# A decoder step on one Trainium2 core: 50 tokens leave the dense expert sum instead of 42, in two gather groups

## The chip, the cores and the metric

The kernel runs on one core of one Trainium2 chip. The metric is the device time of one execution in microseconds (us). The kernel before takes 2029.45 us (median of three runs, 2025.85 to 2030.77). The core's engines are TensorE (PE, matmuls; its weight loads are shown apart as PEld), VectorE (DVE), ScalarE (ACT), GpSimd (POOL) and SyncE (SP). SP's instructions here are DMA issues alone. Each engine works through its own list in order.

## The reference

One layer is computed for 256 prompt tokens and 8 sample tokens (264 in all), width 2048: a projection, a recurrent and an attention half, an output projection with layer norm, then a retrieval layer over 16384 experts. In the retrieval layer every token has 8 heads of 16 experts, 128 in all:

```python
def peer_block(xb, wq, sub_k1, sub_k2, u_tab, v_tab):
    ...
    e = (jnp.take_along_axis(i1, si // PEER_TOPK, axis=-1) * N_KEYS
         + jnp.take_along_axis(i2, si % PEER_TOPK, axis=-1))
    g = jax.nn.softmax(sv, axis=-1)
    ug = u_tab[e]
    act = jax.nn.gelu(jnp.einsum('nd,nhkd->nhk', xb, ug, preferred_element_type=jnp.float32))
    vg = v_tab[e]
    out = jnp.einsum('nhk,nhkd->nd', (g * act).astype(vg.dtype), vg, preferred_element_type=jnp.float32)
```

Both tables have 16384 rows of 2048 fp32 values, 128 MB each. The output is the layer norm of 2^0.25 · x plus this sum, with the keys, values and states of the first half.

## The kernel before

**Two ways to the same sum.** For the first `ND` = 222 tokens ("dense columns") the kernel multiplies with the whole tables: 128 blocks of 128 experts, in each an `up` product (activations of these experts for all dense tokens), gelu, a multiplication with a gate matrix that is zero for experts a token did not choose, and a `down` product. The last `NG` = 42 tokens (34 prompt and 8 sample tokens) are gathered: each stands on `REP` = 3 partitions, each partition has `NJ` = 43 of its 128 experts, and 43 × 2 indirect DMAs of 128 half rows (512 KB) fetch the rows of u, 43 × 2 more those of v.

**Precision by pairs.** A weight block of 512 KB arrives as `raw`; ACT casts its high part (L101, L809) and DVE subtracts to get the low part (L104, L814). Both go with one 444-column matmul (high weights with the high and low half of the operand, 2 × 222 columns: L1202 in `up`, L1247 in `down`) and one 222-column matmul (low weights, high half: L1203, L1249). Each `up` has 16 such pairs, and so has each `down`. In the first six blocks (`NAT`) `up` is plain fp32, on 222 columns (L938).

**The step loop.** Step s does `up(s)`; from s = 34 on (v = s − 34) also `down(v)`, and both add a block's result to `x1` with two DVE sums (`add`, L1255). Steps 0 to 33 run `up` alone; in steps 4 to 20 the gate matrices are made besides, from selections on ACT and DVE and 128-column products, and stored to HBM (`Gd`, 14 stores, L1153). Steps 34 to 127 run both; after them 34 steps run `down` alone (`last_step`), here called the tail. Every eight steps `load_g` loads the gate matrices of eight blocks, 14 DMAs of 64 KB each (L1224).

**Gathers beside the steps.** `gathered()` is a generator, called after each step of v = 0 to 118 as often as a credit of `GRATE` = 1.7 a step allows. A call issues one gather on POOL and uses the one of three calls before (`GDELAY`): for u a dot product with the token's row (L1414), for v an accumulation (L1426, L1428), each one DVE instruction on 1024 elements. At its end 16 matmuls with a selection matrix (L1434) sum the three partitions of each token, and two DVE sums (L1435) add them to `x1`. At its beginning SP loads the expert numbers (`exf`), gate values (`gat`) and the token's rows (`xrep`), 15 DMAs (L1383 to L1385), and DVE makes gather indices of them (`eix`, L1389, L1390).

**What sets the order.** Nothing is reordered: each engine runs the instructions in the order of the code. A weight buffer `raw` (six of them) is loaded again once its low part is subtracted; a pair of high and low parts has one of five slots. SP's DMAs take one of eight completion semaphores in turn, and a DMA waits until the one before it on that semaphore has landed.

Of the kernel before, what the change touches and what calls it, by code (L numbers as in the profile page):

```python
# [47 lines left out]
TRATE = 4  # L48
LEAD = 4
GWAIT = 2  # L50
GRATE = 1.7
GDELAY = 3
EPS = 1e-5
LAM0 = 0.8 - 0.6 * math.exp(-0.0)
# [4 lines left out]
def _build(tc, I, O):  # L59
# [3 lines left out]
    with ctx:  # L63
# [52 lines left out]
        def pmisc(shape):  # L116
            return psum.tile(shape, F32, name="misc", bufs=mmb[0])
# [832 lines left out]
        NEGF = -3.0e38  # L950
        ex = pool_in(ctx, "exp", 1)
        blocks = [(a, 16) for a in range(0, NE, 16)]
        Gd = [dram.tile([128, 128, n], F32, name=f"Gd{a}") for a, n in blocks]
        Ed = dram.tile([SEQ - ND, 128], F32, name="Ed")
        gd = dram.tile([SEQ - ND, 128], F32, name="gd")
        Es = dram.tile([2, NB, 128], F32, name="Es")
# [149 lines left out]
        def tokens(tt):  # L1106
# [19 lines left out]
            for bk, (a0, n) in enumerate(blocks):  # L1126
# [3 lines left out]
                for t4 in range(0, n, 4):  # L1130
# [16 lines left out]
                    def product(a=a, b=b, st=st, t4=t4, w=w, n=n, bk=bk):  # L1147
                        p = psum.tile([128, 4, 128], F32, name="acc2")
                        for q in range(w):
                            nc.tensor.matmul(p[:, q, :], b[:, q, :], a[:, q, :], start=True, stop=True)  # L1150
                        nc.scalar.copy(st[:, :, t4:t4 + w], p[:, :w].rearrange("p t i -> p i t"))
                        if t4 + w == n:
                            nc.sync.dma_start(Gd[bk], st)  # L1153

                    prev.append(product)
                    yield
# [209 lines left out]
        gp = pool_in(ctx, "gath", 1)  # L1366


        eix = gp.tile([128, 2, NJ], I32, name="eix")
        gat = gp.tile([128, NJ], F32, name="gat")  # L1370

        def gathered():
            exf = gp.tile([128, NJ], F32, name="exf")
            selM = cload("selM", [128, NG], pool=gp)
            xrep = gp.tile([128, DM], F32, name="xrep")

            for t in (exf, gat, xrep):
                nc.gpsimd.memset(t, 0.0)
# [10 lines left out]
            nc.vector.tensor_scalar(eix[:, 0], exf, 2.0, None, op0=OP.mult)  # L1389
            nc.vector.tensor_scalar(eix[:, 1], exf, 2.0, 1.0, op0=OP.mult, op1=OP.add)  # L1390
            dots = gp.tile([128, 2, NJ], F32, name="dots")
            yield

# [6 lines left out]
            todo = [(j, a) for j in range(NJ) for a in range(2)]  # L1400

            def ahead(tab, use):
                got = []
                for n in range(len(todo) + GDELAY):
                    if n < len(todo):
                        j, a = todo[n]
                        got.append(rows(tab, a, j))
                    if n >= GDELAY:
                        j, a = todo[n - GDELAY]
                        use(got.pop(0), j, a, slice(a * 1024, (a + 1) * 1024))  # L1410
                    yield

# [76 lines left out]
def _arrays(inp):  # L1489
# [86 lines left out]
```

## Time and profile before

| | us |
|---|---|
| median of three runs | 2029.45 (2025.85 to 2030.77) |
| the profiled execution | 2028.38 |
| its span, first to last instruction | 2026.6 |
| PE busy, PEld busy | 1957.9, 1825.5 |
| DVE busy | 1597.7 |
| ACT busy | 970.9 |
| POOL busy | 343.6 |

The profile is of one execution. Busy time counts an engine's own instructions; a matmul's end is modelled, and matmuls overlap in their pipeline, so the time between starts tells more than the duration of one. The table of stretches gives, for any part of the span, busy time of each engine, the clock granted to TensorE (1.00 is 2.4 GHz, 0.50 is 1.2 GHz), the mean busy share of the 16 DMA engines, and the bytes they moved.

### The profile page before, as it was taken

What the parts mean: (1) busy time and instruction counts of PE and PEld (TensorE: products, weight loads), DVE (VectorE), ACT (ScalarE), POOL (GpSimd) and SP (SyncE); (2) the same over time, 40 slices, a digit from 0 to 9 for tenths busy, and PEclk for the clock granted to TensorE, in tenths of its full rate; (3) what the DMA queues carried; (4) which work ended last, traced back from release to release, by engine and by line L of the source; (5) the groups of instructions that cost most, each with busy time, mean ns of one, the idle gap of its engine ahead of it and who ended that gap; (6) DMA issues with size and microseconds to landing.
All of it is one profiled execution on the core that took longest, in us unless ns stands there. A gap on an engine that the chain in (4) does not pass through costs nothing.

```text
span 2026.6 us, 37121 instructions
## 1 busy us (share of the span) xinstructions
PE 1957.9 (97%) x13874; PEld 1825.5 (90%) x13874; DVE 1597.7 (79%) x2907; ACT 970.9 (48%) x1600; POOL 343.6 (17%) x429
## 2 busy tenths in 40 slices
PE   8999999998999999999999999999999999998995
PEld 8889788797889999999999999999999999997895
DVE  6534656776599888678888888888788888889877
ACT  4224655543211897555454444445554444443443
POOL 2000000004000001012222222222122222223012
PEclk9999899999999999999999999999999999999998
DMA  8899598753344567788988889898788898989661
GB/s 310 298 354 332 184 340 314 271 175 131 125 140 145 192 240 253 262 280 315 322 300 317 301 315 320 287 329 315 269 311 318 300 323 289 327 300 337 230 211 61
DMA packets 179811, 544.18 MB, mean 269 GB/s; under 512 B 22538, under 2 KB 51298, under 8 KB 177586
## 3 DMA queue, kind: packets, MB, share of 16 engines
q1 hardware_dynamic: 150960, 446.92, 63.5%
q0 software_dynamic: 27952, 94.85, 13.2%
q8 instruction: 109, 1.79, 0.3%
q14 instruction: 70, 0.57, 0.1%
q10 hardware_dynamic: 720, 0.05, 0.0%
HBM read 522.19 MB, written 19.54 MB: 267 GB/s over the span
## 4 chain that ended last, share of the span: by engine, by line
PE 79%; DVE 9%; DMA 5%; ACT 4%; issue 2%; SPq 1%; POOL 0%; POOLq 0%; DVEq 0%; ACTq 0%
PE mm L1202 19%; PE acc L1247 19%; PE mm L1203 9%; PE acc L1249 9%; PE mm L938 8%; PE mm L300 3%; PE mm L301 2%; PE mm L302 2%; DMA cv<-in_ck 2%; DVE lo L104 1%; PE acc L1150 1%; DMA cv<-in_cv 1%; PE acc L561 1%; PE acc L640 1%; DVE xrep L1428 1%
## 5 line engine op out<-in xcount | busy, mean ns | idle before, releaser
L104 DVE TENSOR_TENSOR lo<-raw,hi 128x1024 fp32r<-128x1024 f32 x273 | 332.8, 1222 | 77.5 <-ACT hi L101 76.5
L1247 PE MATMUL acc<-w,hi 128*128 128x444 f32 x1224 | 392.8, 374 | 0.0
L101 ACT CAST hi<-raw 128x1024 fp32r<-128x1024 f32 x273 | 284.2, 1045 | 194.6 <-PE acc L1247 141.4
L1202 PE MATMUL mm<-A,hi 128*128 128x444 f32 x1176 | 375.7, 375 | 0.0
L1249 PE MATMUL acc<-w,lo 128*128 128x222 f32 x1224 | 323.7, 264 | 4.6 <-DVE lo L814 4.6
L1203 PE MATMUL mm<-A,lo 128*128 128x222 f32 x1176 | 310.7, 264 | 3.1 <-DVE lo L104 3.1
L1247 PE MATMUL acc<-w,xl 128*128 128x444 f32 x824 | 266.5, 374 | 0.0
L1255 DVE TENSOR_TENSOR M<-M,acc 128x444 f32<-128x444 f32 x256 | 158.2, 618 | 116.5 <-PE acc L1249 108.2
L1202 PE MATMUL mm<-A,xl 128*128 128x444 f32 x776 | 248.4, 375 | 0.0
L1247 PEld LDWEIGHTS acc<-w,hi 128*128 128x128 f32 x1224 | 229.4, 187 | 17.1
L1249 PEld LDWEIGHTS acc<-w,lo 128*128 128x128 f32 x1224 | 233.2, 191 | 8.0 <-DVE lo L814 7.8
L1202 PEld LDWEIGHTS mm<-A,hi 128*128 128x128 f32 x1176 | 220.8, 188 | 16.1
L1203 PEld LDWEIGHTS mm<-A,lo 128*128 128x128 f32 x1176 | 224.7, 191 | 3.3 <-DVE lo L104 3.3
L1249 PE MATMUL acc<-w,xl 128*128 128x222 f32 x824 | 218.8, 266 | 2.8 <-DVE xl L814 2.8
L1203 PE MATMUL mm<-A,xl 128*128 128x222 f32 x776 | 205.2, 264 | 0.0
L101 ACT CAST xl<-raw 128x1024 fp32r<-128x1024 f32 x139 | 145.1, 1048 | 120.3 <-PE acc L1247 100.1
L1396 POOL DMA_INDIRECT ug<-in_u,eix x86 | 118.6, 1379 | 387.7 <-DVE ug L1414 366.7
L104 DVE TENSOR_TENSOR xl<-raw,xl 128x1024 fp32r<-128x1024 f32 x139 | 170.6, 1230 | 15.3 <-ACT xl L101 15.1
L1396 POOL DMA_INDIRECT ug<-in_v,eix x86 | 118.9, 1382 | 344.6 <-DVE xrep L1428 309.4
L1232 ACT CAST w<-ac 128x222 fp32r<-128x222 f32 x128 | 48.5, 379 | 265.5 <-DVE ac L1229 247.9
L1247 PEld LDWEIGHTS acc<-w,xl 128*128 128x128 f32 x824 | 154.9, 188 | 11.5
L1249 PEld LDWEIGHTS acc<-w,xl 128*128 128x128 f32 x824 | 157.4, 191 | 4.8 <-DVE xl L814 4.7
(382 smaller groups left out, 4008.9 us busy)
## 6 DMA issues: line engine op xcount, KB each, us to landing
raw<-in_uT SPq DMA_DIRECT2D x256, 512.0 KB
raw<-in_vt SPq DMA_DIRECT2D x256, 512.0 KB
raw<-in_w_in SPq DMA_DIRECT2D x74, 512.0 KB
cv<-in_ck SPq DMA_DIRECT2D x64, 512.0 KB
cv<-in_cv SPq DMA_DIRECT2D x64, 512.0 KB
raw<-in_wq SPq DMA_DIRECT2D x32, 512.0 KB
Gd<-stage SPq DMA_DIRECT2D x14, 1024.0 KB
gt<-Gd SPq DMA_DIRECT2D x224, 64.0 KB
```

Of the source, the lines that this page charges most:

```text
L101: nc.scalar.copy(hi, raw)
L104: (eng or nc.vector).tensor_tensor(lo, raw, hi, op=OP.subtract)
L300: nc.tensor.matmul(p, hi, xh[:, c], start=c == 0, stop=False)
L301: nc.tensor.matmul(p, hi, xl[:, c], start=False, stop=False)
L938: nc.tensor.matmul(p, w[c // 8][:, c % 8, :], x1[:, c, :n], start=c == 0, stop=c == NC_ - 1)
L1202: nc.tensor.matmul(p, hi[:, c % 8, :], x1s[:, c], start=c == 0, stop=False)
L1203: nc.tensor.matmul(p[:, 0, :], lo[:, c % 8, :], x1s[:, c, 0], start=False, stop=c == NC_ - 1)
L1232: nc.scalar.copy(W[k][:, 0], ac[:, :ND])
L1247: nc.tensor.matmul(p[:, c, :2 * ND].rearrange("p (b t) -> p b t", b=2), hi[:, b % 8, :], w, start=i == 0, stop=False)
L1249: nc.tensor.matmul(p[:, c, :ND], lo[:, b % 8, :], w[:, 0], start=False, stop=i == 7)
L1255: nc.vector.tensor_tensor(a, a, p[:, :, b * ND:(b + 1) * ND], op=OP.add)
L1396: nc.gpsimd.indirect_dma_start(out=t, out_offset=None, in_=tab, in_offset=bass.IndirectOffsetOnAxis(ap=eix[:, a, j:j + 1], axis=0))
```

## The change

The number of gathered tokens goes from 42 to 50, and the dense columns from 222 to 214; `NE`, the padded count of gate columns, stays 224. The gathered tokens form two groups: the 42 of before (now `t0` = 222), three partitions each, 43 experts a partition; then eight prompt tokens (`t0` = 214) on 16 partitions each, eight experts a partition. The groups run one after the other in one generator, so the second has its own loads (16 × 3 DMAs), indices, 16 + 16 gathers and reduction. The credit is 2.2 a step while s < 128 and 0.7 in the tail. The gate matrices lie in one HBM tensor in the order in which they are loaded: a store writes runs of 512 B, and one DMA of 7 KB a partition loads eight blocks.

```diff
-NG = 42
+NG = 50
 ND = T - NG
-REP = 128 // NG
-NJ = -(-128 // REP)
+
+GROUPS = [(a, n, 128 // n, -(-128 // (128 // n))) for a, n in ((T - 42, 42), (ND, NG - 42))]
+NJ = max(g[3] for g in GROUPS)
...
-GRATE = 1.7
+GRATE = 2.2
+GTAIL = 0.7
...
-        Gd = [dram.tile([128, 128, n], F32, name=f"Gd{a}") for a, n in blocks]
+        Gd = dram.tile([128, 16, len(blocks), 128], F32, name="Gd")
...
-                            nc.sync.dma_start(Gd[bk], st)
+                            nc.sync.dma_start(Gd[:, :, bk], st.rearrange("p (g i) t -> p g (i t)", i=8))
...
-            for bk, (a0, n) in enumerate(blocks):
-                nc.sync.dma_start(gts[g][:, 8 * a0:8 * (a0 + n)], Gd[bk][:, g * 8:(g + 1) * 8, :])
+            nc.sync.dma_start(gts[g], Gd[:, g].rearrange("p b x -> p (b x)"))
...
-        def gathered():
+        def gathered(t0, n, rep, nj, k):
...
-            for r in range(REP):
-                a, b, e = r * NG, r * NG + SEQ - ND, (r + 1) * NG
-                c, d = r * NJ, min((r + 1) * NJ, 128)
+            np_ = max(0, min(n, SEQ - t0))
+            for r in range(rep):
+                a, b, e = r * n, r * n + np_, (r + 1) * n
+                c, d = r * nj, min((r + 1) * nj, 128)
                 for k, (i, o) in enumerate(((Ed, exf), (gd, gat))):
-                    nc.sync.dma_start(o[a:b, :d - c], i[:, c:d])
-                    nc.sync.dma_start(o[b:e, :d - c], Es[k][:, c:d])
-                nc.sync.dma_start(xrep[a:e], xgd)
+                    nc.sync.dma_start(o[a:b, :d - c], i[t0 - ND:t0 - ND + np_, c:d])
+                    if b < e:
+                        nc.sync.dma_start(o[b:e, :d - c], Es[k][:, c:d])
+                nc.sync.dma_start(xrep[a:e], xgd[t0 - ND:t0 - ND + n])
...
-        gg = gathered()
+        gg = (_ for k, g in enumerate(GROUPS) for _ in gathered(*g, k))
         credit = 0.0
         for v in range(128):
             step(v + RUN)
-            credit += GRATE
+            credit += GRATE if v + RUN < 128 else GTAIL
```

Three places show how the instructions move. The line numbers of the changed kernel are up to eight higher. The first place is SP's list around v = 82. Before, only weight halves stand there (`raw<-in_uT` for `up`, `raw<-in_vt` for `down`), and then the gate loads of v = 83:

```order
L88 DMA raw<-in_uT 128x1024 [waits DMAHW3_49,DVE_49]
L88 DMA raw<-in_uT 128x1024 [waits DMAHW4_49,DVE_49]
L1188 DMA raw<-in_vt 128x1024 [waits DMAHW5_49,DVE_49]
L1188 DMA raw<-in_vt 128x1024 [waits DMAHW6_49,DVE_49]
L88 DMA raw<-in_uT 128x1024 [waits DMAHW7_49,DVE_49]
```

Now, on SP at the same place, behind the two `raw<-in_vt` of v = 82:

```order
L1191 DMA raw<-in_vt 128x1024 [waits DMAHW3_49,DVE_49]
L1191 DMA raw<-in_vt 128x1024 [waits DMAHW4_49,DVE_49]
L1388 DMA exf<-Ed 8x8 [waits DVE_49]
L1388 DMA gat<-gd 8x8 [waits DMAHW5_49]
L1391 DMA xrep<-xgd 8x2048 [waits DMAHW6_49,PE_49]
L1388 DMA exf<-Ed 8x8 [waits DMAHW7_49]
L1388 DMA gat<-gd 8x8 [waits DMAHW0_49]
```

The three loads `exf`, `gat`, `xrep` stand there sixteen times, and only then come the four weight halves of v = 83; the first `xrep` waits for PE (the reduction, which reads the buffer it overwrites), and DMAHW0 to DMAHW7 are the eight completion semaphores.

The second place is DVE's list from the end of step v = 82 (its last accumulation, L1434) to the beginning of v = 84 in the changed kernel; L106 and L816 subtract low parts, L1257 are the sums of `down`, L1442 the reduction's sums:

```order
L1434 SCALAR_TENSOR_TENSOR xrep<-ug,exf,xrep 128x1024
L1442 TENSOR_TENSOR M<-M,misc 128x8x42 x2
L106 TENSOR_TENSOR lo<-raw,hi 128x1024
L1257 TENSOR_TENSOR M<-M,acc_19246 128x2x214 x2
L106 TENSOR_TENSOR xl<-raw,xl 128x1024
L1217 TENSOR_TENSOR ac<-ac,mm 128x214
L1231 TENSOR_TENSOR ac<-ac,gt 128x224
L816 TENSOR_TENSOR xl<-raw,xl 128x1024
L1238 TENSOR_TENSOR w<-ac,w 128x214
L106 TENSOR_TENSOR lo<-raw,hi 128x1024
L1395 TENSOR_SCALAR eix<-exf 128x8
L1396 TENSOR_SCALAR eix<-exf 128x8
```

The reduction's sums and the index arithmetic of the second group now stand amid the full steps; before, both stood at the two ends of the gathers alone (v = 1 and v = 107). The next row behind them is the low part of the first weight half for `down` of v = 84.

The third place is DVE's list in the tail. Before, most steps have two accumulations (L1428):

```order
L814 TENSOR_TENSOR lo<-raw,hi 128x1024
L1236 TENSOR_TENSOR w<-ac,w 128x222
L814 TENSOR_TENSOR xl<-raw,xl 128x1024
L1428 SCALAR_TENSOR_TENSOR xrep<-ug,exf,xrep 128x1024 x2
L1255 TENSOR_TENSOR M<-M,acc_20663 128x2x222 x2
L1229 TENSOR_TENSOR ac<-ac,gt 128x224
```

Now, in the tail of the changed kernel, a step has one (L1434) or none:

```order
L816 TENSOR_TENSOR lo<-raw,hi 128x1024
L1238 TENSOR_TENSOR w<-ac,w 128x214
L816 TENSOR_TENSOR lo<-raw,hi 128x1024
L1434 SCALAR_TENSOR_TENSOR xrep<-ug,exf,xrep 128x1024
L1257 TENSOR_TENSOR M<-M,acc_21278 128x2x214 x2
L1231 TENSOR_TENSOR ac<-ac,gt 128x224
L816 TENSOR_TENSOR xl<-raw,xl 128x1024
L1238 TENSOR_TENSOR w<-ac,w 128x214
L816 TENSOR_TENSOR xl<-raw,xl 128x1024
L1257 TENSOR_TENSOR M<-M,acc_21332 128x2x214 x2
```

In the tail 16 accumulations remain, in the steps v = 94 to 115, and the second reduction stands at v = 117; before, accumulations went on to v = 106 at 1.7 a step, and the reduction stood at v = 107.

## Rows read from the trace of the kernel before

**Rows 1.** The page's engine totals: busy us, share of the span, instructions.
```profile
span 2026.6 us, 37121 instructions
...
PE 1957.9 (97%) x13874; PEld 1825.5 (90%) x13874; DVE 1597.7 (79%) x2907; ACT 970.9 (48%) x1600; POOL 343.6 (17%) x429
```
**Rows 2.** Stretches: length, busy PE, PEld, DVE, ACT, POOL (instructions), clock, DMA share, GB/s.
```profile
100.00:150.00 50.00, 45.86 (x584) 41.12 (x582) 17.39 (x31) 10.87 (x15) 2.70 (x5) 0.97 0.94 358
...
675.00:788.00 113.00, 111.54 (x828) 107.98 (x827) 100.94 (x264) 106.48 (x246) 1.42 (x10) 1.00 0.70 241
...
868.00:1799.00 931.00, 931.00 (x5948) 890.07 (x5947) 802.90 (x1075) 463.08 (x654) 222.37 (x243) 1.00 0.88 308
950.00:1050.00 100.00, 100.00 (x640) 95.61 (x640) 86.95 (x125) 49.65 (x70) 24.68 (x27) 1.00 0.88 308
...
1831.00:1880.00 49.00, 44.14 (x259) 38.39 (x257) 48.71 (x63) 17.42 (x24) 17.07 (x13) 1.00 0.96 336
1897.00:1951.00 54.00, 54.00 (x346) 51.55 (x346) 45.64 (x66) 25.54 (x34) 0.00 (x0) 1.00 0.64 215
```
**Rows 3.** Timeline of PE, 160 to 164 us: start, duration, line; one in three left.
```profile
161.38 0.28 PE L301 MATMUL mm<-xl,A 128*128 128x264 f32 x1
...
163.55 0.28 PE L301 MATMUL mm<-xl,A 128*128 128x264 f32 x1
```
**Rows 4.** Groups of PE, 641 to 675 us: count, then busy us, mean ns, idle.
```profile
L938 PE MATMUL mm<-M,raw 128*128 128x222 f32 x160 | 30.6, 352 | 0.0
```
**Rows 5.** Groups of instructions, 950 to 1400 us, the same columns.
```profile
L1414 DVE SCALAR_TENSOR_TENSOR ug<-ug,xrep 128x1024 f32<-128x1024 f32 x77 | 91.5, 1220 | 0.0
...
L1255 DVE TENSOR_TENSOR M<-M,acc 128x444 f32<-128x444 f32 x90 | 55.7, 618 | 47.4 <-PE acc L1249 43.1 <-PE acc L1247 2.8
...
L1414 DVE DVE_READ_ACCUMULATOR ug<-ug,xrep 128x1 f32 x77 | 6.4, 83 | 0.0
```
**Rows 6.** Timeline of PE in the tail: first matmul of v = 94, reduction, v = 108.
```profile
1809.76 0.38 PE L1247 MATMUL acc<-w,xl 128*128 128x444 f32 x1
...
1892.72 3.67 PE L1434 MATMUL misc<-c_selM,xrep 128*128 128x42 f32 x32
1896.22 0.45 PE L1247 MATMUL acc<-w,hi 128*128 128x444 f32 x1
```
**Rows 7.** Groups of instructions in the tail, 1831 to 1880 us.
```profile
L1428 DVE SCALAR_TENSOR_TENSOR xrep<-ug,exf,xrep 128x1024 f32<-128x1024 f32 x14 | 17.4, 1279 | 0.0
```
**Rows 8.** Timeline of SP's DMA issues: first, eighth, twelfth and last of the 15 loads.
```profile
876.07 0.31 SPq L1383 DMA_DIRECT2D exf<-Ed  x1
...
882.00 0.23 SPq L1383 DMA_DIRECT2D gat<-gd  x1
...
883.42 0.26 SPq L1384 DMA_DIRECT2D exf<-Es  x1
...
884.80 0.31 SPq L1385 DMA_DIRECT2D xrep<-xgd  x1
```
**Rows 9.** Timeline of DVE: the index arithmetic; in brackets the wait before, its end.
```profile
886.34 0.19 DVE L1389 TENSOR_SCALAR eix<-exf 128x43 int32<-128x43 f32 x1 [2.31 <-DMA exf<-Es]
```
**Rows 10.** Stretches with an idle PE, and behind one; columns as in rows 2.
```profile
499.00:504.00 5.00, 0.25 (x2) 0.00 (x0) 4.90 (x8) 0.80 (x2) 0.00 (x0) 1.00 0.00 0
505.00:511.00 6.00, 5.01 (x12) 3.88 (x13) 5.86 (x10) 5.16 (x10) 0.00 (x0) 0.50 0.00 1
799.00:803.00 4.00, 0.94 (x6) 0.64 (x5) 3.80 (x10) 1.57 (x3) 0.00 (x0) 1.00 1.00 384
```
**Rows 11.** DMA issues of the page: count, KB each.
```profile
Gd<-stage SPq DMA_DIRECT2D x14, 1024.0 KB
gt<-Gd SPq DMA_DIRECT2D x224, 64.0 KB
```
**Rows 12.** GB/s in 40 equal slices of the stretch 1800 to 1890 us.
```profile
GB/s 342 384 355 408 406 259 259 211 255 269 280 306 311 381 362 249 243 353 354 249 342 371 328 421 417 382 300 350 295 328 377 381 317 344 310 251 228 268 264 138
```

More of the change, by code (lines that the diff above doesn't have):

```diff
@@ L1366, in _build @@
         gp = pool_in(ctx, "gath", 1)
-        eix = gp.tile([128, 2, NJ], I32, name="eix")
-        gat = gp.tile([128, NJ], F32, name="gat")
-        def gathered():
+        def gathered(t0, n, rep, nj, k):
+            eix = gp.tile([128, 2, NJ], I32, name="eix")
+            gat = gp.tile([128, NJ], F32, name="gat")
             exf = gp.tile([128, NJ], F32, name="exf")
-            selM = cload("selM", [128, NG], pool=gp)
+            selM = cload(f"selM{k}", [128, n], pool=gp)
             xrep = gp.tile([128, DM], F32, name="xrep")
-            for t in (exf, gat, xrep):
-                nc.gpsimd.memset(t, 0.0)
-            for r in range(REP):
-                a, b, e = r * NG, r * NG + SEQ - ND, (r + 1) * NG
-                c, d = r * NJ, min((r + 1) * NJ, 128)
+            if rep * n < 128:
+                nc.gpsimd.memset(xrep, 0.0)
+            if rep * n < 128 or rep * nj > 128:
+                for t in (exf, gat):
+                    nc.gpsimd.memset(t, 0.0)
+            np_ = max(0, min(n, SEQ - t0))
+            for r in range(rep):
+                a, b, e = r * n, r * n + np_, (r + 1) * n
+                c, d = r * nj, min((r + 1) * nj, 128)
                 for k, (i, o) in enumerate(((Ed, exf), (gd, gat))):
-                    nc.sync.dma_start(o[a:b, :d - c], i[:, c:d])
-                    nc.sync.dma_start(o[b:e, :d - c], Es[k][:, c:d])
-                nc.sync.dma_start(xrep[a:e], xgd)
+                    nc.sync.dma_start(o[a:b, :d - c], i[t0 - ND:t0 - ND + np_, c:d])
+                    if b < e:
+                        nc.sync.dma_start(o[b:e, :d - c], Es[k][:, c:d])
+                nc.sync.dma_start(xrep[a:e], xgd[t0 - ND:t0 - ND + n])
             for _ in range(GWAIT):
                 yield
-            nc.vector.tensor_scalar(eix[:, 0], exf, 2.0, None, op0=OP.mult)
-            nc.vector.tensor_scalar(eix[:, 1], exf, 2.0, 1.0, op0=OP.mult, op1=OP.add)
+            nc.vector.tensor_scalar(eix[:, 0, :nj], exf[:, :nj], 2.0, None, op0=OP.mult)
+            nc.vector.tensor_scalar(eix[:, 1, :nj], exf[:, :nj], 2.0, 1.0, op0=OP.mult, op1=OP.add)
             dots = gp.tile([128, 2, NJ], F32, name="dots")
@@ L1398, in rows @@
                 return t
-            todo = [(j, a) for j in range(NJ) for a in range(2)]
+            todo = [(j, a) for j in range(nj) for a in range(2)]
             def ahead(tab, use):
                 got = []
-                for n in range(len(todo) + GDELAY):
-                    if n < len(todo):
-                        j, a = todo[n]
+                for m in range(len(todo) + GDELAY):
+                    if m < len(todo):
+                        j, a = todo[m]
                         got.append(rows(tab, a, j))
-                    if n >= GDELAY:
-                        j, a = todo[n - GDELAY]
+                    if m >= GDELAY:
+                        j, a = todo[m - GDELAY]
                         use(got.pop(0), j, a, slice(a * 1024, (a + 1) * 1024))
@@ L1417, in gathered @@
             yield from ahead(I["u"], dot)
-            wts = gp.tile([128, NJ], F32, name="exf")
-            nc.vector.tensor_tensor(wts, dots[:, 0], dots[:, 1], op=OP.add)
+            wts = gp.tile([128, NJ], F32, name="exf")[:, :nj]
+            nc.vector.tensor_tensor(wts, dots[:, 0, :nj], dots[:, 1, :nj], op=OP.add)
             nc.scalar.activation(wts, wts, AF.Gelu_apprx_tanh)
-            nc.vector.tensor_tensor(wts, wts, gat, op=OP.mult)
+            nc.vector.tensor_tensor(wts, wts, gat[:, :nj], op=OP.mult)
             accg = gp.tile([128, DM], F32, name="xrep")
@@ L1431, in gathered @@
             for h in (0, 8):
-                pf = pmisc([128, 8, NG])
+                pf = pmisc([128, 8, n])
                 for c in range(8):
                     nc.tensor.matmul(pf[:, c, :], accg[:, (h + c) * 128:(h + c + 1) * 128], selM, start=True, stop=True)
-                nc.vector.tensor_tensor(x1[:, h:h + 8, ND:], x1[:, h:h + 8, ND:], pf, op=OP.add)
-        gg = gathered()
+                y = x1[:, h:h + 8, t0:t0 + n]
+                nc.vector.tensor_tensor(y, y, pf, op=OP.add)
+        gg = (_ for k, g in enumerate(GROUPS) for _ in gathered(*g, k))
         credit = 0.0
@@ L1543, in _arrays @@
     r = np.arange(128)
-    a["selM"] = (r[:, None] % NG == np.arange(NG)[None, :]).astype(f) * (r[:, None] < NG * REP).astype(f)
+    for k, (_, n, rep, _) in enumerate(GROUPS):
+        a[f"selM{k}"] = (r[:, None] % n == np.arange(n)[None, :]).astype(f) * (r[:, None] < n * rep).astype(f)
     return a
```

## The prediction

> **What bounds the kernel now.** First the engine totals [rows 1]: TensorE (PE) is busy 97% of the span, VectorE (DVE) 79%. Those are averages, so next the table of stretches [rows 2]. In the stretch 868 to 1799 us, where each step runs one `up` and one `down`, PE has no gap at all (931.00 of 931.00 us) and makes 5948 matmuls, that is 2974 pairs of a 444-column and a 222-column matmul: 0.313 us a pair, 10.02 us a step of 32 pairs. DVE is busy 802.90 us there, 86%. From 1831 to 1880 us, in the tail where only `down` is left, DVE is busy 48.71 of 49 us and PE waits; from 1897 to 1951 us, with the gathers over, PE is full again and DVE takes 45.64 of 54 us. From 675 to 788 us ScalarE (ACT) is busy 106.48 of 113 us and sets the pace. So a narrower pair pays wherever PE is full, and the extra DVE work pays nothing only where DVE has room.
>
> **Pairs.** Dense columns go from 222 to 214, so a pair streams 642 columns, not 666. What a column costs is read from matmuls of another width: 18 matmuls of 264 columns take 163.55 − 161.38 = 2.17 us [rows 3], 0.1206 us each, 0.457 ns a column; the pair now costs 0.313/666 = 0.470 ns a column. 24 columns at 0.457 are 11 ns. Bounds: 7.3 ns if the short matmul does not shrink (16 columns), 11.3 ns at 0.470; zero belongs to a rival below. There are (122 + 128) × 16 = 4000 pairs; the 15 steps 6 to 19 and 21 (240 pairs) wait for ACT or DVE, the other 3760 gain 11 ns: **−41.4 us** (−27 to −42.5). The step becomes 9.66 us, a tail step 4.83 us. The plain fp32 `up` of steps 0 to 5 takes 30.6 us for 160 of its 192 records [rows 4]: 36.7 × 8/222 = **−1.3 us**.
>
> **More gathers, in the long steps.** 172 gathers become 204; the rate goes from 1.7 to 2.2 calls a step, so five steps carry 2, 2, 2, 2, 3. One dot costs DVE 1.220 us and its accumulator read some 0.08 [rows 5]. 86.95 us of DVE in 100 us [rows 2] is 8.71 us a step at 1.7 gathers; half a gather more makes 9.36 us of 9.66. A step with three has 6.5 + 3 × 1.30 = 10.4 us, 0.74 too much, and the four others have 0.56 to spare each. I price this at nothing: DVE runs ahead, as 47.4 us of waiting for PE before the 90 sums of line 1255 show [rows 5], and PE would need that lead used up. If the cover fails, each of the 17 such steps costs 0.74 us.
>
> **Tail.** The loop's step v = 94 begins at 1809.76 and v = 108 at 1896.22 us [rows 6]: 14 steps in 86.5 us, where 14 × 5.01 = 70.1 would do. So 16.3 us are lost to DVE, 3.5 of them to the reducing matmuls of line 1434. Afterwards 16 accumulations fall in 24 tail steps. DVE needs 45.64/54 × 5.01 = 4.23 us without a gather, less 0.05 for the narrower operands, plus 0.67 × 1.24 (17.4 us for 14 of them [rows 7]): 5.0 us against PE's 4.83, some 4.5 us over 24 steps, of which DVE's lead covers part. I take 2, plus 3.5 for the second group's reduction: the loss falls from 16.3 to 5.5, **−10.8 us** (−8 to −13).
>
> **The seam between the groups.** At v = 82 the first group is reduced amid the full steps: 32 matmul records, 3.5 us of PE [rows 6], **+3.5**. In the same call SyncE (SP) gets 48 small loads, of which the third waits for that reduction; behind them stand the next steps' weight loads. Now 15 such loads take from 876.07 to 885.11 us [rows 8] (the last starts at 884.80 and takes 0.31), 0.60 us each with weights still arriving, and 0.40 us each in the run of seven from 882.00 to 884.80. With no gathers in flight I take 0.38, near the second. Counting from the start of step 82 on PE: down ends at 9.7 us, the reduction at 13.2, the 46th load (the last of expert numbers) is issued at about 29.6 and lands about 2.9 later, as the one issued at 883.42 is the last that DVE waits for, until 886.34 [rows 8, 9]: 32.5 us. DVE reaches the index arithmetic at about 21 and stands there; behind it is the low half that `down` of step 84 needs at 27.7. It comes at 34, the next one after the two sums 1.2 us too late as well: PE stops 7.5 us. At 0.33 us a load it would be 5, at 0.60 some 17. Now the same wait of DVE (2.31 us [rows 9]) costs PE nothing, because it is shorter than the lead. **+7.5 us** (5 to 17).
>
> PE stands still some 6 us there. After its idle stretch of 499 to 504 us the granted clock was 0.50, that is 1.2 GHz, from 505 to 511 us; after the stretch 799 to 803, with 0.94 us of work, it stayed at 1.00 [rows 10]. I take 2 us for a spell at half clock (0 to 3.4). The Trainium skill (TensorE: Matmul & The Clock Gate, section "Why this matters for your kernels") says that gaps between bursts of matmuls drop the clock to half; the first of these stretches agrees, the second does not, and by the rule the term is +2, by the second stretch 0. **+2 us**.
>
> **Gate matrices.** The 14 stores are now cut into 512 B runs and the 224 loads become 16 of 7 KB runs. The loads take SP and the transfer engines less: between nothing and a few us of gain in the tail, counted as nothing. The stores lie in 675 to 788 us at a DMA share of 0.70 [rows 2], about half of it theirs (one store of 1 MB a step [rows 11] against two weight halves of 512 KB). If short runs cost as much per byte: nothing. At twice the cost the share is 1.05 and the 113 us grow by 6. I take nothing, since 0.3 of the share is free; three times is a rival.
>
> **Sum.** −41.4 − 1.3 − 10.8 + 3.5 + 7.5 + 2 = −40.5 us on the profiled execution's own 2028.38 us (span 2026.6): 1987.9. The median of the runs shown is 1.1 us above that execution: **1989 us**.
>
> **Rivals.**
> *Weight loads set the pace.* The loading of weights (PEld) is busy 95.61 of 100 us [rows 2] and 128 columns of weights load in every half of a pair, whatever the dense width. Then pairs gain nothing: 1989 + 41.4 = 2030, no change. Against it: the 264-column stream loads weights for each matmul too, and does one in 0.1206 us [rows 3], where a pair has 0.156 per load. The Trainium skill (Trainium Kernel Development and Optimization, section "Performance Expectations") calls the busy share of weight loads, not that of matmuls, the good measure of nearness to the limit, and by it this is the case; the trace's 264-column stream contradicts. Chance 0.05.
> *DVE becomes the bound in three-gather steps*: 17 × 0.74 = +12.6 us, 2002. For it: DVE at 97%, gathers landing close to use. Against: the lead. 0.09.
> *The seam costs little* (5 or less in all, since DVE's lead or the landing is better): 1977. 0.10.
> *DMA becomes the bound, and the kernel slower.* A step moves 4 × 0.524 + 2.2 × 0.524 + 0.115 = 3.37 MB; in 9.66 us that is 348 GB/s. For it: 308 GB/s at a share of 0.88 and 336 at 0.96 both extrapolate to 350 [rows 2]. Against: 358 GB/s at a share of 0.94 from 100 to 150 us [rows 2], and 2.25 us slices up to 428 in the tail [rows 12]. The gain is eaten when a step reaches 9.66 + 40.5/94 = 10.09 us, a ceiling of 333 GB/s; at 325 the step is 10.4 us and the time 2056. 0.06.
> *Short-run stores at three times the cost*: share 1.4, the 113 us grow by some 45, 2034. At 1.7 to 2.5 times 1990 to 2020. 0.06.
>
> **How the numbers follow.** The forecast has 0.64, with 1976 to 2004 as its own range: pairs 7.3 ns instead of 11 add 14 us, the seam at 17 adds 10, a small seam takes 12. The range 1974 to 2008 takes in the seam and DVE rivals; left out are weight loads 0.05, most of DMA and stores 0.10, and some 0.04 below. This kernel's runs can tell about 0.3%, 6 us, from no change. Slower by more: DMA 0.05 and stores 0.01, so 0.06; within: weight loads 0.05 and 0.01 of the others, 0.06; faster: 0.88.
>
> **What would show it.** PE in the full stretch without gaps and about 0.302 us a pair; a step of 9.66 us; DVE at 95 to 97% there; one hole of PE of 5 to 10 us near v = 84, ended by DVE and before it by the loads of expert numbers, with clock 0.5 behind it; tail steps of 4.8 to 5.0 us; the steps of 675 to 788 us as long as now. Wrong would be: pairs still at 0.313, PE waits for weight tiles all along the full stretch (DMA), or longer steps before 790 us (stores).

## The result and the profile after

The changed kernel takes 2001.61 us (median of four runs, 1999.87 to 2002.6) beside 2027.65 us before in the same job: a ratio of 0.9877, 95% interval 0.9859 to 0.9895. It is faster by 1.2%. The forecast was 1989 us with a range of 1974 to 2008: the sign and the range held, but of the 40.5 us forecast, 27.0 us show between the two profiled spans (2026.6 and 1999.6 us). The time also is that of the DVE rival (2002 us), but not for its reason, as shown below.

The engine totals of the page after, to be held against [rows 1]:

```profile
span 1999.6 us, 37148 instructions
...
PE 1931.7 (97%) x13906; PEld 1834.9 (92%) x13906; DVE 1623.9 (81%) x2961; ACT 964.2 (48%) x1601; POOL 405.0 (20%) x461
```

Stretches of the profile after (length, busy PE, PEld, DVE, ACT, POOL with instructions, granted clock, DMA share, GB/s). The first four answer to [rows 2], the last four lie at the two reductions:

```profile
675.00:785.00 110.00, 108.01 (x812) 105.96 (x811) 100.00 (x260) 103.79 (x239) 1.42 (x10) 1.00 0.78 246
865.00:1666.00 801.00, 801.00 (x5241) 784.63 (x5240) 747.43 (x998) 403.48 (x576) 267.41 (x254) 1.00 0.94 342
950.00:1050.00 100.00, 100.00 (x656) 97.93 (x655) 93.95 (x137) 50.07 (x72) 35.58 (x35) 1.00 0.94 342
...
1679.80:1683.00 3.20, 3.20 (x13) 3.08 (x13) 2.89 (x5) 0.00 (x0) 0.00 (x0) 0.50 0.17 46
1696.50:1700.40 3.90, 0.00 (x0) 0.00 (x0) 1.40 (x4) 0.00 (x0) 0.95 (x1) 0.96 0.64 160
1700.40:1703.50 3.10, 3.07 (x11) 2.91 (x12) 3.06 (x6) 1.26 (x2) 2.77 (x2) 0.50 0.95 365
1800.00:1900.00 100.00, 100.00 (x655) 97.77 (x654) 98.45 (x138) 45.43 (x60) 11.33 (x12) 1.00 0.84 295
...
1915.20:1921.90 6.70, 6.70 (x26) 6.47 (x27) 4.25 (x7) 2.27 (x3) 0.00 (x0) 0.50 0.28 94
```

PE is full from 865 to 1666 us, with 5241 matmuls: 0.3057 us a pair, where 0.302 was forecast. DVE is busy 94% of the hundred us from 950, and PE has no gap, so the steps with three gathers cost nothing. The tail is full too (1800 to 1900 us), and DVE's 98.45 us there are hidden. Steps 6 to 21, where the first row lies, take 133.2 us beside 132.6 before (table below): the stores do not show.

The same as a balance of stages, from the first matmul of each stage to that of the next:

| stage | before, us | after, us | difference |
|---|---|---|---|
| start to step 6 | 675.2 | 672.2 | -3.0 |
| steps 6 to 21 | 132.6 | 133.2 | +0.7 |
| steps 22 to 33 (`up` alone) | 60.1 | 58.6 | -1.5 |
| v = 0 to 81 (full steps) | 821.6 | 802.3 | -19.3 |
| v = 82 to 84 (the seam) | 30.1 | 40.2 | +10.1 |
| v = 85 to 93 | 90.2 | 88.1 | -2.1 |
| v = 94 to 126 (tail) | 183.9 | 170.7 | -13.2 |
| the rest | 32.9 | 34.1 | +1.2 |

The head and the end are no effects that these profiles resolve: step 6 begins anywhere from 668.3 to 677.2 us in the kernels below with the same head as after, at 670.5 and 671.1 in two with the same head as before, and step 21 takes 8.3 to 9.9 us in kernels of the one kind and 8.5 to 11.4 in those of the other.

The seam went as worked out. PE after (start, duration, instruction, in brackets the idle time before):

```profile
1676.23 3.81 PE L1440 MATMUL misc<-c_selM,xrep 128*128 128x42 f32 x32
1679.83 0.71 PE L1205 MATMUL mm<-A,hi 128*128 128x428 f32 x1
...
1696.07 0.38 PE L1249 MATMUL acc<-w,hi 128*128 128x428 f32 x1
1700.43 0.55 PE L1251 MATMUL acc<-w,lo 128*128 128x214 f32 x1 [3.99 <-DVE lo L106]
```

DVE after, at the same place:

```profile
1686.25 1.23 DVE L106 TENSOR_TENSOR lo<-raw,hi 128x1024 fp32r<-128x1024 f32 x1 [0.23 <-ACT hi L103]
1699.00 0.17 DVE L1395 TENSOR_SCALAR eix<-exf 128x8 int32<-128x8 f32 x1 [11.53 <-DMA gat<-gd]
...
1699.16 1.22 DVE L106 TENSOR_TENSOR lo<-raw,hi 128x1024 fp32r<-128x1024 f32 x1
```

And SP after, whose list holds the 48 loads:

```profile
1673.71 0.29 SPq L1388 DMA_DIRECT2D exf<-Ed  x1
1674.05 0.29 SPq L1388 DMA_DIRECT2D gat<-gd  x1
1680.07 0.26 SPq L1391 DMA_DIRECT2D xrep<-xgd  x1
...
1696.44 0.29 SPq L1388 DMA_DIRECT2D gat<-gd  x1
1696.78 0.29 SPq L1391 DMA_DIRECT2D xrep<-xgd  x1
```

Read backwards: PE waits 3.99 us for a low part, DVE makes it only after the index arithmetic, which waited 11.53 us for the last of these loads (by the trace the last gate values, issued 0.33 us behind the last expert numbers), and that one is issued at 1696.44 us because SP stood at the third load until the reduction was over (1680.07) and then needed 0.37 us for each in the mean. Step v = 82 begins on PE at 1666.4 us, so the index arithmetic comes 32.6 us later (forecast 32.5).

### The profile page after: what moved, and what is told of

The parts are those of the page before. It is cut to its first block, busy times and chain, and to the rows that moved or that the text cites. A ratio compares the mean times of both kernels' runs of the same rounds, so it can differ in the third digit from the quotient of the medians.

```text
span 1999.6 us, 37148 instructions
## 1 busy us (share of the span) xinstructions
PE 1931.7 (97%) x13906; PEld 1834.9 (92%) x13906; DVE 1623.9 (81%) x2961; ACT 964.2 (48%) x1601; POOL 405.0 (20%) x461
## 3 DMA queue, kind: packets, MB, share of 16 engines
q8 instruction: 109, 1.79, 0.4%
## 4 chain that ended last, share of the span: by engine, by line
PE 82%; DVE 6%; DMA 6%; ACT 4%; issue 1%; SPq 1%; POOL 0%; POOLq 0%; ACTq 0%; DVEq 0%
PE acc L1249 21%; PE mm L1205 18%; PE acc L1251 10%; PE mm L1206 9%; PE mm L940 8%; PE mm L302 3%; PE mm L304 2%; PE mm L303 2%; DMA cv<-in_ck 2%; DMA cv<-in_cv 2%; DVE lo L106 1%; PE acc L1153 1%; PE acc L642 1%; PE acc L563 1%; PE misc L381 1%
## 5 line engine op out<-in xcount | busy, mean ns | idle before, releaser
L106 DVE TENSOR_TENSOR lo<-raw,hi 128x1024 fp32r<-128x1024 f32 x273 | 332.9, 1222 | 76.6 <-ACT hi L103 76.4
L1249 PE MATMUL acc<-w,hi 128*128 128x428 f32 x1224 | 387.2, 373 | 0.0
L1205 PE MATMUL mm<-A,hi 128*128 128x428 f32 x1176 | 369.2, 372 | 0.0
L1251 PE MATMUL acc<-w,lo 128*128 128x214 f32 x1224 | 321.0, 262 | 4.0 <-DVE lo L106 4.0
L1206 PE MATMUL mm<-A,lo 128*128 128x214 f32 x1176 | 308.0, 262 | 3.3 <-DVE lo L106 3.3
L1249 PE MATMUL acc<-w,xl 128*128 128x428 f32 x824 | 261.4, 371 | 0.0
L1205 PE MATMUL mm<-A,xl 128*128 128x428 f32 x776 | 242.6, 371 | 0.0
L1251 PE MATMUL acc<-w,xl 128*128 128x214 f32 x824 | 216.4, 263 | 0.0
L1206 PE MATMUL mm<-A,xl 128*128 128x214 f32 x776 | 202.5, 261 | 0.0
L1257 DVE TENSOR_TENSOR M<-M,acc 128x428 f32<-128x428 f32 x256 | 153.5, 600 | 41.3 <-PE acc L1251 36.8
L106 DVE TENSOR_TENSOR xl<-raw,xl 128x1024 fp32r<-128x1024 f32 x139 | 170.5, 1229 | 15.3 <-ACT xl L103 15.3
L1249 PEld LDWEIGHTS acc<-w,xl 128*128 128x128 f32 x824 | 155.5, 189 | 5.6
```

The lines of the kernel that those rows point to most:

```text
L106: (eng or nc.vector).tensor_tensor(lo, raw, hi, op=OP.subtract)
L1205: nc.tensor.matmul(p, hi[:, c % 8, :], x1s[:, c], start=c == 0, stop=False)
L1206: nc.tensor.matmul(p[:, 0, :], lo[:, c % 8, :], x1s[:, c, 0], start=False, stop=c == NC_ - 1)
L1249: nc.tensor.matmul(p[:, c, :2 * ND].rearrange("p (b t) -> p b t", b=2), hi[:, b % 8, :], w, start=i == 0, stop=False)
L1251: nc.tensor.matmul(p[:, c, :ND], lo[:, b % 8, :], w[:, 0], start=False, stop=i == 7)
L1257: nc.vector.tensor_tensor(a, a, p[:, :, b * ND:(b + 1) * ND], op=OP.add)
```

## The experiments

**Widths of the two matmuls.** In `up` and `down`, steps v = 0 to 92:

```diff
-                nc.tensor.matmul(p, hi[:, c % 8, :], x1s[:, c], start=c == 0, stop=False)
-                nc.tensor.matmul(p[:, 0, :], lo[:, c % 8, :], x1s[:, c, 0], start=False, stop=c == NC_ - 1)
+                m, n = wide(k - RUN) if c else (2 * ND, ND)
+                nc.tensor.matmul(p.rearrange("p b t -> p (b t)")[:, :m], hi[:, c % 8, :],
+                                 x1s[:, c].rearrange("p b t -> p (b t)")[:, :m], start=c == 0, stop=False)
+                nc.tensor.matmul(p[:, 0, :n], lo[:, c % 8, :], x1s[:, c, 0, :n], start=False, stop=c == NC_ - 1)
...
-        gg = gathered()
+        gg = iter(())
```

> The kernel before, with the gathered tokens' expert sum left out, and with narrower matmuls in the full steps v = 0 to 92: every three steps another pair of widths (wide 444 down to 268 beside a short one of 222; short 222 down to 126 beside a wide one of 444; then 428/214, 412/206, 396/198), so the sums of the dropped columns are left out too. Read from the trace, start to start. Known so far: wide 212.2 ns at 444 and 207.8 at 428 (4.4 ns for 16 columns), short 101.1 at 222 and 97.7 at 214. Theory of the prediction, that a column costs 0.457 ns everywhere: wide 190 ns at 396 and 132 at 268, short 90 at 198. Theory now, that the wide matmul gives back only 0.28 ns a column: wide 199 at 396 and 163 at 268, short 0.42 ns a column. Rival, that weight loads set the pace: the wide one falls, the short one stands still below some width, and the sum of a pair has a floor.

PE in three steps of this run: first 444 beside 222, then 396 beside 222, then 444 beside 126 (rows with the start of a wide matmul, of the short one behind it, and of the eighth or twelfth wide one after that):

```profile
792.22 0.37 PE L1209 MATMUL mm<-A,xl 128*128 128x444 f32 x1
792.43 0.26 PE L1211 MATMUL mm<-A,xl 128*128 128x222 f32 x1
...
794.71 0.37 PE L1209 MATMUL mm<-A,hi 128*128 128x444 f32 x1
...
1132.65 0.35 PE L1209 MATMUL mm<-A,hi 128*128 128x396 f32 x1
1132.83 0.27 PE L1211 MATMUL mm<-A,lo 128*128 128x222 f32 x1
...
1136.15 0.35 PE L1209 MATMUL mm<-A,hi 128*128 128x396 f32 x1
...
1635.02 0.41 PE L1209 MATMUL mm<-A,hi 128*128 128x444 f32 x1
1635.27 0.22 PE L1211 MATMUL mm<-A,lo 128*128 128x126 f32 x1
...
1638.78 0.42 PE L1209 MATMUL mm<-A,xl 128*128 128x444 f32 x1
```

(794.71 - 792.22)/8 = 0.311 us a pair; (1136.15 - 1132.65)/12 = 0.292; (1638.78 - 1635.02)/12 = 0.313. So 48 columns off the wide matmul give 21 ns, and 96 columns off the short one nothing. The start of the short matmul hides it: beside 126 columns it comes 0.25 us after the wide one instead of 0.21, and the next wide one 0.06 us after it. Medians over all such pairs of the run, start to start:

| wide / short | 444/222 | 444/214 | 444/174 | 444/126 | 428/222 | 428/214 | 396/222 | 396/198 | 268/222 |
|---|---|---|---|---|---|---|---|---|---|
| pair, ns | 313 | 313 | 312 | 312 | 306 | 305 | 292 | 293 | 235 |

(Of the 81 pairs at 444/126 nine, each the first behind a pair that is not narrowed, take only 264 to 273 ns and draw the mean to 308; the others take 306 to 320.) The prediction's price (0.457 ns for every column) fails, and so does the theory of 0.28 ns a wide column, which read the delay of the short matmul as part of the wide one. A wide column gives 0.44 ns ((313 - 235)/176). The rival with a floor stands.

**Narrower weights and wider short matmuls.** The same kernel with a weight width for each of the two matmuls:

```diff
+                m, n, e, f = wide(k - RUN) if 0 < c < NC_ - 1 else (2 * ND, ND, 128, 128)
+                q, x = p.rearrange("p b t -> p (b t)"), x1s[:, c].rearrange("p b t -> p (b t)")
+                nc.tensor.matmul(q[:e, :m], hi[:, c % 8, :e], x[:, :m], start=c == 0, stop=False)
+                nc.tensor.matmul(q[:f, :n], lo[:, c % 8, :f], x[:, :n], start=False, stop=c == NC_ - 1)
```

> The kernel before without the gathered tokens' expert sum; in the full steps v = 0 to 89 the middle pairs of each product have other widths or narrower weights, every three steps another, so sums of dropped columns and experts are left out or wrong. The run with narrowed columns showed: pair 313 ns at 444/222, still 313 at 444/126, 292 at 396/222, 236 at 268/222; so the short matmul's width gives nothing and a wide column 0.44 ns. Theory: the next wide matmul's weights (128 columns) load under the short stream and take longer than it, some 118 ns. Then the pair stands at 313 up to a short width of about 265 to 285 and grows 0.44 ns a column beyond (318 to 335 at 318, 340 to 350 at 350); with 64 columns of weights for the wide matmul alone it falls toward the stream, 280 to 292 ns; with 64 for the short one alone it stays 313; equal widths below 264 all make about 236 to 240 a pair. Rival, that every matmul has a fixed cost apart from its weights' load: narrower weights change nothing, 313 in all of them.

PE with 64 columns of weights for the wide matmul (`128*64`), then with both matmuls 160 columns wide and full weights:

```profile
1330.15 0.36 PE L1213 MATMUL mm<-A,xl 128*64 128x444 f32 x1
1330.35 0.26 PE L1214 MATMUL mm<-A,xl 128*128 128x222 f32 x1
...
1332.58 0.36 PE L1213 MATMUL mm<-A,xl 128*64 128x444 f32 x1
...
1700.11 0.28 PE L1213 MATMUL mm<-A,hi 128*128 128x160 f32 x1
1700.22 0.28 PE L1214 MATMUL mm<-A,lo 128*128 128x160 f32 x1
...
1701.90 0.28 PE L1213 MATMUL mm<-A,hi 128*128 128x160 f32 x1
```

2.43/8 = 0.304 us and 1.79/8 = 0.224 us a pair. Means over the run:

| case | pair, ns | wide, short |
|---|---|---|
| 444/222, 64 weight columns for the wide matmul | 302.9 | 202.5, 100.4 |
| 444/222, 64 for the short one | 312.3 | 210.6, 101.7 |
| 444/126, 64 for the wide one | 261.8 | 204.6, 57.2 |
| 444/246, full weights | 316.7 | 204.3, 112.4 |
| 444/286, full weights | 335.0 | 204.0, 131.0 |
| 264/264 | 244 | 122, 122 |
| 222/222, 190/190, 160/160 (medians) | 223 each | 112, 112 |

So a matmul with 128 columns of weights behind it takes 111.5 ns at least, at 222, 190 and 160 columns alike: that is the next matmul's weight load. Only the load for the wide matmul, which runs beside the short stream, matters; narrowed, it frees the short one (57 ns at 126 columns). The short stream of 222 columns needs 101 ns and so lies 10 ns below the floor; from 246 columns on it is above it. The rival of a fixed cost falls, since narrower weights did change the time. Of my own numbers the floor was too high (118 for 111.5), and with it the width at which it ends (265 to 285 for 246) and the gain of narrower weights (280 to 292 expected, 303 measured).

**The credits alone.**

```diff
-GRATE = 1.7
+GRATE = 2.2
+GTAIL = 0.7
...
-            credit += GRATE
+            credit += GRATE if v + RUN < 128 else GTAIL
```

> The kernel before, 42 gathered tokens in one group and 222 dense columns, with only the credits of the change (2.2 a step, 0.7 in the tail), so that all gathers lie in full steps and the reduction falls at v = 82. Theory: the 16.3 us that the tail loses now go, the reduction costs 3.6 us amid the full steps and 1.7 us for a spell at half clock behind it: 11 us less, about 2016.5, full steps still 10.02 us. Rival, that the full steps pay for more gathers (steps with three at 10.4 us): 17 steps with three cost up to 7 us and the time is about 2024.

2014.39 us, ratio 0.9933 (0.9918 to 0.9948): 13.6 us less, where 11 were expected; in its profile the tail is 17.3 us shorter than before and v = 82 to 84 3.6 us longer. Its reduction and the stretch of the tail that was DVE's before [rows 2]:

```profile
1684.90:1698.50 13.60, 13.60 (x99) 13.15 (x97) 7.33 (x10) 6.18 (x9) 0.10 (x1) 1.00 0.44 160
1831.00:1880.00 49.00, 49.00 (x317) 47.08 (x316) 40.82 (x60) 22.25 (x29) 0.00 (x0) 1.00 0.70 234
```

PE is full in the tail, full steps still take 10.02 us, the reduction's step 13.5 and no clock falls behind it. So about half of what the change brings needs none of its tokens.

**The place of the gate matrices alone.**

```diff
-        Gd = [dram.tile([128, 128, n], F32, name=f"Gd{a}") for a, n in blocks]
+        Gd = dram.tile([128, 16, len(blocks), 128], F32, name="Gd")
...
-                            nc.sync.dma_start(Gd[bk], st)
+                            nc.sync.dma_start(Gd[:, :, bk], st.rearrange("p (g i) t -> p g (i t)", i=8))
...
-            for bk, (a0, n) in enumerate(blocks):
-                nc.sync.dma_start(gts[g][:, 8 * a0:8 * (a0 + n)], Gd[bk][:, g * 8:(g + 1) * 8, :])
+            nc.sync.dma_start(gts[g], Gd[:, g].rearrange("p b x -> p (b x)"))
```

> The kernel before with only the change of the gate matrices' place in HBM (stores in runs of 512 B, loads of 7 KB runs). Theory: no change, within 2 us of 2027.65, steps 6 to 19 still 8.58 us. Rival, that short runs cost more per byte: steps 8 to 18 longer, 6 to 45 us more. Second rival, that fewer gate loads in SP's list bring something in the tail: up to 3 us less.

2026.34 us, ratio 0.9995 (0.9984 to 1.0006): no change, and most of the steps 6 to 18 still take 8.58 us. The store rival falls, and so does the second one: the tail takes 183.9 us as before.

**The second group left out.**

```diff
-        gg = (_ for k, g in enumerate(GROUPS) for _ in gathered(*g, k))
+        gg = gathered(*GROUPS[0], 0)
```

> The changed kernel with the second group left out: the sum of these eight tokens over their experts is computed nowhere. 214 dense columns, first reduction at v = 82 as in the changed kernel. Theory: the 4.0 us hole at v = 84 with its 1.7 us of half clock and the 6.75 us around the second reduction go, nothing else: 12.4 us less than the changed kernel's 2001.6, about 1989; pairs stay at 0.306 us everywhere. Rival, that gathers lengthen the pairs by their traffic: pairs at 0.302 us in the steps after v = 84, where no gathers are left, and 1 to 5 us less again.

1986.54 us, ratio 0.9792 (0.9776 to 0.9808), against 0.9877: 15 to 17 us less than the changed kernel, somewhat more than the 12.4 expected. In its profile the seam takes 34.5 us instead of 40.2 and the tail 164.0 instead of 170.7, together the 12.4 us, and v = 0 to 81 and 85 to 93 are as long as in the changed kernel. What the median gains besides must lie at the two ends, which vary from one profile to the next; its cause is not shown. Full steps are 9.78 us with 2.2 gathers and 9.79 without any, so the gathers' traffic doesn't lengthen pairs. The step of the reduction takes 13.30 us and the next one, at half clock for 3.4 us, 11.46; then the steps are 9.78 at once: the hole belongs to the second group's loads.

**Few large loads.** For the second group, three DMAs in place of 48:

```diff
-            for r in range(rep):
+            if np_ == n:
+                m = 128 // nj
+                for i, o in ((Ed, exf), (gd, gat)):
+                    x = i[t0 - ND:t0 - ND + n]
+                    st = [list(y) for y in x.ap]
+                    nc.sync.dma_start(o[:m * n, :nj], bass.AP(tensor=x.tensor, offset=x.offset, ap=[[nj, m], st[0], [1, nj]]))
+                    if m < rep:
+                        nc.sync.dma_start(o[m * n:rep * n, :128 - m * nj], x[:, m * nj:])
+                nc.sync.dma_start(xrep[:rep * n], bcast(xgd[t0 - ND:t0 - ND + n], rep))
+            for r in range(0 if np_ == n else rep):
```

> The changed kernel with one edit: the second group's expert numbers, gate values and token rows come by three DMAs instead of 48, the numbers first; the token rows still wait for the first reduction. Theory: DVE's wait of 11.5 us for the numbers goes, with it PE's hole of 4.0 us at v = 84 and the 1.7 us of half clock behind it: 5.7 us less, about 1996. Rival, that SP's stand of 6 us at the reduction, with weight loads queued behind it, makes the hole: it stays, 2001.

1991.0 us, ratio 0.9834 (0.9818 to 0.985). SP and DVE of this run at the seam:

```profile
1670.31 0.76 SPq L1389 DMA_DIRECT2D gat<-gd  x1
1675.88 0.52 SPq L1392 DMA_DIRECT2D xrep<-xgd  x1
1677.56 2.62 SPq L90 DMA_DIRECT2D raw<-in_uT  x2
```

```profile
1682.06 1.23 DVE L106 TENSOR_TENSOR lo<-raw,hi 128x1024 fp32r<-128x1024 f32 x1 [0.23 <-ACT hi L103]
1683.20 0.16 DVE L1404 TENSOR_SCALAR eix<-exf 128x8 int32<-128x8 f32 x1
```

SP stands nearly as long for the reduction (4.8 us until 1675.88, where it was 5.7), the index arithmetic waits for nothing, and PE has no hole: v = 82 to 84 take 34.5 us instead of 40.2. SP's stand by itself is not the cause, the numbers' lateness is. The edit does two things, fewer loads and all numbers ahead of the stand; which of them it takes, no run separates. The 5.7 us at the seam are what was expected. In this profile the second reduction, too, costs less, 3.6 us instead of 6.75, since no clock fell behind it; that is about the rest of the gain.

**Reductions between the pairs.** Three of the runs vary this; in the first two DVE's sum stands right behind the eighth matmul:

```diff
-            for h in (0, 8):
-                pf = pmisc([128, 8, n])
-                for c in range(8):
-                    nc.tensor.matmul(pf[:, c, :], accg[:, (h + c) * 128:(h + c + 1) * 128], selM, start=True, stop=True)
+            sums.extend((one, c) for c in range(16))
+            while sums:
+                yield
...
                 nc.tensor.matmul(p[:, 0, :], lo[:, c % 8, :], x1s[:, c, 0], start=False, stop=c == NC_ - 1)
+                some()
```

> As the one before, and the 16 matmuls of each reduction are put one behind each of the next 16 pairs instead of in a block (a credit of 2.25 instead of 2.2 a step keeps the second one before the end). Theory: the blocks of small matmuls are what drops the clock; the 1.7 us of half clock behind the first and the 3.1 us behind the second go too: about 1991. The 3.6 us that each reduction takes from PE stay. Rival, that the clock falls after any reduction: still about 1996; or that each small matmul between two pairs costs more than 0.23 us: above 1996.

1995.95 us, ratio 0.9852 (0.9833 to 0.9871): no gain over the run with few loads, nor the 1991 us expected. DVE's waits from 1650 to 1690 us (in all, times, longest):

```profile
DVE M L1462 <- PE misc L1459: 10.0, 2, 6.2
```

The theory left out that DVE stands in order: the sum amid `up` holds up the low parts behind it, PE then waits 1.5 us and runs at half clock. Moving the two sums to the end of the step takes that away:

```diff
             while sums:
                 yield
+            for h in (0, 8):
+                y = x1[:, h:h + 8, t0:t0 + n]
+                nc.vector.tensor_tensor(y, y, pf[h // 8], op=OP.add)
```

> The changed kernel with few large loads and 50 tokens; the 16 matmuls of each reduction stand one behind each of the 16 next pairs, as in the interleaved run, but DVE's two sums stand at the end of that step, not amid it (credit 2.25). In the interleaved run DVE stood 6.2 and 3.7 us for the two sums and PE waited 1.5 us for DVE behind them. Theory: without that wait no gap, and no spell at half clock: 1.7 us under the run with few loads, about 0.982 of before. Rival, that the small matmuls drop the clock in any place: 0.983 as the run with few loads; or that DVE waits for the reduction here too: 0.985.

1989.46 us, ratio 0.9832 (0.9809 to 0.9855). No gap, no fall of the clock (steps of 13.39 and 9.79 us), but 1.7 us are too little to be told from the run with few loads.

> As the one before with 52 tokens gathered: ten in the second group, on twelve partitions each, 212 dense columns, credit 2.4. Theory: the wide matmul is 4 columns narrower, 3760 pairs by 1.8 ns, 6.9 us less, about 1984, because DVE still has room (6.5 + 2.4 x 1.3 = 9.6 us in a step of about 9.73). By the prediction's price (0.457 ns for all 6 columns) 10 us less, 1981. Rival, that DVE is the bound: steps at 9.8 us or longer and no gain, 1990 or above.

1993.96 us, ratio 0.985 (0.9827 to 0.9872): inconclusive, since it carries the same stand of DVE (a step of 16.76 us); its full steps are 9.74 us. Its forecast (1984 us) was missed.

**More tokens.** The kernel with few loads (`exf` and `gat` cleared before `xrep`) with other constants, beside the changed kernel once more:

```diff
-NG = 50
+NG = 54
...
-GRATE = 2.2
+GRATE = 2.45
```

> The changed kernel once more, beside the next three: 0.988 of before.

2000.88 us, ratio 0.988 (0.9857 to 0.9903). In this profile no clock fell behind the first reduction, and the hole was larger (PE's waits at the seam):

```profile
PE acc L1251 <- DVE lo L106: 5.9, 1, 5.9
```

> The changed kernel with the few large loads, and 52 tokens gathered (ten in the second group, twelve partitions each; 212 dense columns; credit 2.35). By the price that the narrowed columns gave (wide matmul 0.455 ns a column, short one nothing): pair 1.8 ns less, 3760 pairs, 6.9 us under the run with few loads and 50 tokens, 0.980 of before. By the prediction's price 2.7 ns a pair, 10 us. Rival, that DVE or the transfer engines are the bound now: steps 9.78 us or longer, 0.983 or more.

> As the one before with 54 tokens gathered (twelve in the second group on ten partitions each; 210 dense columns; credit 2.45). A pair of 0.302 us makes a step of 9.67 us; DVE needs 6.5 + 2.45 x 1.3 = 9.69 us, so it is the edge. If DVE's lead carries: 0.977 of before. Rival, that DVE sets the pace: steps of 9.7 to 9.8 us with waits of PE for DVE, no gain over 52 tokens, 0.980 or more. Second rival, the transfer engines: 2.45 gathers a step make 3.49 MB in 9.67 us, 361 GB/s, and PE waits for weights.

1988.01 us (0.9826, 0.9806 to 0.9847) with 52, 1983.2 us (0.9797, 0.9778 to 0.9816) with 54 tokens. Both stayed short of their forecasts (0.980 and 0.977): with 52 tokens the full steps take 9.74 us, 1.3 ns less a pair where 1.8 were expected. 54 is the fastest here, 17.7 us under the changed kernel of the same job. Of its full steps, 500 us, then the 90 us behind them and one PE row in those (idle time in brackets):

```profile
1000.00:1500.00 500.00, 500.00 (x3309) 495.11 (x3309) 483.02 (x648) 248.91 (x363) 203.29 (x174) 1.00 0.97 356
1500.00:1590.00 90.00, 89.69 (x595) 88.05 (x595) 85.56 (x104) 44.61 (x66) 28.95 (x29) 1.00 0.93 343
...
1535.87 0.36 PE L1251 MATMUL acc<-w,lo 128*128 128x210 f32 x1 [0.17 <-DVE lo L106]
```

Up to 1500 us it is 0.3022 us a pair and no gap, with DVE at 97% and 356 GB/s. From 50 to 54 tokens the step falls from 9.785 to 9.67 us: 3.6 ns a pair for eight wide columns, 0.45 a column. But then DVE's lead runs out: in the next 90 us three short matmuls come late (0.3 us of idle PE, the largest piece a wait for DVE), and the steps v = 67 and 69 take 10.03 and 10.12 us. So 54 tokens at this credit reach DVE's edge near the end of the first group's gathers; where the transfers become the bound stays open.

## Why the prediction was right in sign and short in size

| term | forecast, us | measured, us |
|---|---|---|
| pairs, 3760 | -41.4 (11 ns each) | -27.6 (7.35 ns each) |
| seam | +13.0 | +10.9 |
| tail | -10.8 | -9.6 |
| native `up`; all that is left | -1.3 | -0.7 |

The pair is the 19.3 us of v = 0 to 81 over 2624 pairs; the seam 40.21 less three steps of 9.785; the tail the 6.75 lost now less the 16.3 of before. The last row is what remains of the 27.0 us and is not resolved.

**Pairs: the step that failed.** "24 columns at 0.457 are 11 ns." The price of a column was right for the wide matmul: 16 columns at 0.457 are 7.3 ns, the lower bound that I had written down for the case that the short one does not shrink, and that case is the real one. I set it aside with the argument against the rival on weight loads, "the 264-column stream loads weights for each matmul too, and does one in 0.1206 us, where a pair has 0.156 per load". That compares a mean over two unlike matmuls with a floor that holds for each: 0.1206 us is above the floor of 0.1115, and the short matmul's 0.101 below it (the pair's 0.313 [rows 2] less 0.212 from the start of the wide matmul to that of the short one; 0.21 in the first rows of the widths run). And a stream just above the floor says nothing on one below it. The rival as I put it (nothing gained) was wrong as well: the wide matmul lies far above the floor (195 ns at 428 columns, as 0.3057 less 0.111 says).

The Trainium skill (TensorE: Matmul & The Clock Gate, section "LDWEIGHTS (loading the stationary operand)") gives the load's time as the weight columns divided by 1.2, in ns: 107 for 128 columns, whatever their rows. The runs come near it: 111.5 measured, and with 64 columns the floor is gone. Set against the 101 ns of the short matmul, that sentence would have given 7.3 ns and, with the other terms as they were, an estimate of 2003 us. The other rule, on the busy share of weight loads (Trainium Kernel Development and Optimization, section "Performance Expectations"), pointed at the right engine part, but here its share did not measure the distance: at 95.6% [rows 2] a pair took 313 ns, and the same two loads took 223 ns beside matmuls of 160 to 222 columns.

**More gathers.** Right: hidden in the full steps at 2.2 and 2.35 a step, and at 2.45 until DVE's lead ran out at v = 67. The total of 2002 that the DVE rival gave is a coincidence; its 17 steps of 10.4 us are not there.

**Tail.** The accumulations cost nothing (I took 2). The second reduction cost 6.75 instead of 3.5: near the end of its 32 records the clock fell to 0.50, for 6.8 us. Without that fall, in the run with few loads, it cost 3.6.

**Seam.** The times at which DVE came to the index arithmetic and at which it could go on were right within 0.1 us, the second in part by luck: the last numbers were issued 0.1 us later than forecast, and the load that ended the wait another 0.33 us later but with a shorter landing (2.6 for 2.9 us). The hole was 4.0 instead of 7.5 us. PE came to the place 30.0 us after the start of v = 82 and not 27.7, mostly since 3.4 us behind the reduction ran at half clock (1.6 us), and also since full steps are 9.785, not 9.66 us, and one wide matmul of `down` could run before the low part was needed; that is 2.3 us of the difference, and the second wait of 1.2 us did not come. In the second profile of the same kernel, where that spell was missing, the hole was 5.9 us and the seam as long (40.8 against 40.2 us). The spells of half clock were forecast as 2 us behind the hole; they came behind each reduction as well, in some profiles.

**Gate matrices.** Right, nothing.

## What to carry to other kernels

Price a narrower matmul by its own start-to-start time against the floor that the next matmul's weight load sets, matmul by matmul; a mean over a pair hides the one that is under it. Before small loads are multiplied, look who stands in order behind their first user: three DMAs for 48, the numbers first, were worth 5.7 us at the seam beside the 26 us of the whole change. And try the schedule alone before the data: moving gathers out of the tail gave half.

## What the runs showed of the hardware

A matmul with a full load of 128 fp32 weight columns behind it took 111.5 ns or more, from 222 columns down to 160 the same; a column above the floor cost 0.43 to 0.46 ns at a granted clock of 1.00. PEld's records of such a load say 0.19 us each in all these cases, so their busy share (98% of the stretch) is no measure of the floor. And the clock fell to 0.50 near the end of a block of 32 reducing records or right behind it, with no gap of PE, in 8 of the 14 such blocks of the profiles here; behind the first reduction it did so in one profile of the changed kernel and not in the other. That cost 1.6 us behind a first reduction and 3.2 behind a second one. What decides it is not shown.
